# One vector sum of the SwiGLU weights queued behind an addition to a matmul bank

## The chip, the cores and the metric

The kernel runs on one core of a Trainium2 chip. A core has five engines that run side by side, each with its own queue worked off in order: TensorE (PE in the profile; its weight loads are PEld), VectorE (DVE), ScalarE (ACT), GpSimd (POOL) and SyncE (SP), which here issues most transfers. The metric is the time of one execution on the device in microseconds (us), lower is better.

## The reference, cut to what matters

One decoder block on 512 tokens of width 1024 in float32. Two token mixers (a gated convolution and a gated linear recurrence) are merged, and a SwiGLU channel mixer follows, with `D_FF = 2816`:

```python
x = x + m @ w_mix_out[l]
h = rmsnorm(x, norm2_g[l])
x = x + (jax.nn.silu(h @ ffn_w1[l]) * (h @ ffn_w3[l])) @ ffn_w2[l]
return rmsnorm(x, norm_f_g)
```

The change is in the products `h @ ffn_w1` and `h @ ffn_w3`.

## The kernel before, in words

**Products.** Float32 operands are split into a high part `h` and a low part `l`, and each product is made of three matmuls (high by high, low by high, high by low). Weights arrive by DMA in a buffer `raw`; ScalarE casts the high part (line 122) and VectorE, in this stage, subtracts to get the low part (line 118). Four `raw` buffers, two `wsum` buffers and five `hl` buffers (a split piece of weights) rotate.

**Seven products for eight.** The columns of `ffn_w1` and `ffn_w3` are worked in 11 pairs `k`, each pair being columns `j` and `j + 11` of both matrices in pieces of 128. Pair 0 is done plainly. The ten others use a scheme of the Strassen kind: the weights of a pair are seen as quarters `b11`, `b12`, `b21`, `b22`, and four sums of them, `t1` to `t4`, are made, so that seven products do (`b11`, `t1`, `b21`, `t2`, `t4`, `b22`, `t3`). Each product is 24 matmuls of 256 columns on line 1053. `f_sum` makes the sums in place: `t1 = b12 + b11` and `t2 = t1 + b22` by VectorE (line 346), `t3` by a subtraction, `t4` by an accumulating DMA that GpSimd issues (line 344).

**The banks.** The results meet in PSUM banks. The product `t1` is copied to a buffer `se`, the common sum, from its bank `fe` (line 1149). `t2` accumulates into the bank of `b11` (`fr` or `fa`), which is copied into a new bank `ft` (line 1144). Then `b22` accumulates into the old bank and `t3` into the new one. Behind `b22`, `se` is added to the old bank (line 1151, by the helper `add` of line 879). Behind `t3`, the bank is added to `se` (line 1153, same helper; in the profile `se<-ft,se`), and the result is gated by Silu on ScalarE (line 1110, `sl`) and a multiplication on VectorE (line 1111, into `ou` or `ov`). `t4` accumulates into the bank of `t3` and is gated likewise.

**The order.** The products are traced in this list, in which `t4` of a pair comes two products or so behind its `t3`, after the next pair has begun:

```python
for k, before in zip(F_PAIRS, [None] + F_PAIRS):
    F_ORDER += [(n, k) for n in ("b11", "t1", "b21", "t2") if n[0] == "t" or k not in BEGUN]
    if before is not None:
        F_ORDER.append(("t4", before))
    F_ORDER += [("b22", k), ("t3", k)]
F_ORDER.append(("t4", F_PAIRS[-1]))
```

For pairs 1 to 4 (`BEGUN`) the products `b11` and `b21` were done before this loop. Each product, when it asks for its weights, has the loads and sums of weights traced up to four pieces further on (`AHEAD = 4`); the sum `t1` is traced there, by `source` in `f_chunk`.

**Who orders the queues.** Outside a few stretches written by hand, a planner decides at build time the order of instructions in each engine's queue, from its own estimates of when each is ready. An instruction can be held behind another of the same engine by `tc.issue_after(ins)`, which fixes the order only and adds no wait for a result. `newest` is a dictionary of instructions for such edges; before the change it holds `load` and `sub`.

**Behind this stage** the products with `ffn_w2` follow (line 926, bank `or`), by the same scheme with `e`, `u`, `v` operands, with sums of weights that were made earlier and lie in DRAM (`os`). They end in the last norm and the store of the output.

Of the kernel before, what the change touches and what calls it, by code (L numbers as in the profile page):

```python
# [85 lines left out]
def tile_block(ctx, tc, a, out):  # L86
# [19 lines left out]
    def bank(name):  # L106
        return psum.tile([P, T], F32, tag="mm", name=name)
# [7 lines left out]
    newest = {}  # L115

    def sub(eng, o, x, y):
        return eng.tensor_tensor(out=o, in0=x, in1=y, op=ALU.subtract)  # L118
# [18 lines left out]
    def wchunk(key, src, kt, cols, where="hl", lo=pool_e, after=None):  # L137
        chunks.append((key, src, kt, cols, where, lo, after))
# [190 lines left out]
    def f_load(n, k, raw=None):  # L329
        if raw is None:  # L330
            p_, tag = (wsums, "wsum") if n in ("b12", "b22") else (raws, "raw")
            raw = p_.tile([P, 1024], F32, tag=tag, name=f"raw_f{n}_{k}")
        for i, w_ in enumerate((w1, w3)):
            nc.sync.dma_start(raw[:, i * T : (i + 1) * T].rearrange("p (k n) -> p k n", k=4), f_quarter(n, k, w_, 0, 4))
        f_raw[n, k] = raw

    def f_sum(n, k):

        o, x = {"t1": ("b12", "b11"), "t2": ("b12", "b22"), "t3": ("b11", "t2"), "t4": ("b21", "t2")}[n]
        q, y = f_raw[o, k], f_raw[x, k]  # L340
        if n == "t3":
            sub(vec, q, y, q)
        elif n == "t4" or k in ADDING:
            pool_e.dma_start(out=q, in_=y, accum_op=ALU.add)  # L344
        else:
            vec.tensor_tensor(out=q, in0=q, in1=y, op=ALU.add)  # L346
        f_raw[n, k] = q

    def f_chunk(n, k):

        again = k in BEGUN

        def source():
            if n in ("b11", "b21"):
                f_load(n, k)
                if n == "b11" and not again:
                    f_load("b12", k)
            elif n == "t1":
                for m in ("b11", "b12", "b22", "b21") if again else ("b22",):
                    f_load(m, k)  # L360
                f_sum("t1", k)
            return f_raw[n, k]

        def after(rv, h):
            if n == "t1":
                f_sum("t2", k)
                f_sum("t3", k)
                if again:
                    f_sum("t4", k)
            elif n == "b21" and not again:  # L370
                f_sum("t4", k)

        wchunk(f"f{n}_{k}", source, 8, P, "made", vec, after)
# [490 lines left out]
    for j in range(8):  # L864
        ws = w_tiles(f"lo{j}_0", 5) + w_tiles(f"lo{j}_1", 5)
        ps = bank(f"yb{j}")
# [12 lines left out]
    add = lambda o, x, y: vec.tensor_tensor(out=o, in0=x, in1=y, op=ALU.add)  # L879
# [100 lines left out]
    for n, j in enumerate(mixq.order()):  # L980
        ws = w_tiles(f"co{j}", ND)
        ps = bank(f"ya{j}")
# [64 lines left out]
    def f_product(ps, k, x_, w_, again=False, ahead=AHEAD):  # L1047

        h, l = weights(f"f{w_}_{k}", ahead)
        for i in range(2):  # L1050
            for c, (xh, xl) in enumerate(x_):
                for m, (lw, rx_) in enumerate(((h, xh), (h, xl), (l, xh))):
                    pe.matmul(  # L1053
                        ps[:, HALVES[i]], lw[:, 4 * i + c, :], rx_, start=not (again or i or c or m),
                        stop=bool(i and c == 3 and m == 2), skip_group_check=True,
                    )
# [51 lines left out]
    def f_out(c, dst, sign=1.0):  # L1108
        s_ = shortt("sl")
        act.activation(s_[:, LO], c[:, LO], AF.Silu, scale=sign)  # L1110
        vec.scalar_tensor_tensor(out=dst, in0=c[:, HI], scalar=sign, in1=s_[:, LO], op0=ALU.mult, op1=ALU.mult)
# [21 lines left out]
    def ffn_product(n, k):  # L1133

        b_ = seven.setdefault(k, {"a": first[k][0]} if k in BEGUN else {})
        x_ = {"b11": "a11", "b21": "a12", "b22": "s4", "t1": "s1", "t2": "s2", "t3": "s3", "t4": "a22"}[n]
        r = {"b11": "a", "b21": "b", "b22": "a", "t1": "e", "t2": "a", "t3": "c", "t4": "c"}[n]
        if n in ("b11", "t1"):
            b_[r] = (bank2 if r == "e" else bank)(f"f{r}_{k}")
        ps = b_[r]  # L1140
        f_product(ps, k, f_in[x_], n, n not in ("b11", "t1"))
        if n in ("b11", "t2"):
            new = b_["b" if n == "b11" else "c"] = bank(f"f{n}_{k}")
            act.copy(new, ps)
            if n == "b11":
                o7.uv[k] = longt(f"ou{k}"), longt(f"ov{k}")
        elif n == "t1":
            b_["se"] = shortt(f"se_{k}")
            act.copy(b_["se"], ps)
        elif n == "b22":  # L1150
            add(ps, ps, b_["se"])
        elif n == "t3":
            add(b_["se"], ps, b_["se"])
        if n not in ("b11", "t1", "t2"):
            i, cs = {"b21": (0, LO), "b22": (0, HI), "t3": (1, HI), "t4": (1, LO)}[n]
            f_out(b_["se"] if n == "t3" else ps, o7.uv[k][i][:, cs], -1.0 if n in ("b22", "t3") else 1.0)
        if n == "t4" and k >= SUMS_FROM:
            o7.pair(k - SUMS_FROM)

    for n, k in F_ORDER:  # L1160
        ffn_product(n, k)
# [95 lines left out]
```

## Time and profile before

| what | value |
| --- | --- |
| median of 3 runs | 806.26 us (805.32 to 806.38) |
| profiled execution | 806.61 us |
| its span, first to last instruction | 804.8 us |
| mean granted TensorE clock | 0.994 |
| busy: PE, DVE, ACT, POOL | 98%, 84%, 59%, 29% |
| sums of line 346 | 20, 1.23 us each, 493.2 to 663.8 us |
| additions `se<-ft,se` | 10, 0.68 us each, 522.9 to 689.8 us |

The profiled execution's own time is 1.8 us more than its span. The profile gives, for each instruction, its engine, line, operation, and the tiles that it writes and reads (`out<-in`), and for an idle time of an engine what released it. A chain of waits follows the work that ended last backwards, step by step. Matmuls are pipelined: the length shown for one (0.28 us for 256 columns) is longer than the distance from one to the next (0.12 us). The granted clock is the share of full speed that TensorE was given.

### The profile page before, as it was taken

The page shows a single profiled execution, that of the slowest core. Times are in us where ns is not written, and L with a number is a line of the kernel's source. Part 1 is how long each engine was busy: PE and PEld are TensorE (multiplying, and loading weights), DVE is VectorE, ACT ScalarE, POOL GpSimd, SP SyncE. Part 2 cuts the span into 40 slices and gives each one's busy share as a digit, 9 for nine tenths or more (in the row PEclk, how much of TensorE's full clock was granted, in tenths as well). Part 3 has the DMA queues.
Part 4 walks back from the last instruction along what each step waited for, and adds up shares of the span by engine and source line. Part 5 has one row for each costly group of instructions (what it writes and reads, how often), then busy time and mean ns, then how long its engine had stood idle before and what let it go on. Part 6 is the DMA issues. An engine that isn't in the chain of part 4 may idle for free.

```text
span 804.8 us, 12198 instructions
## 1 busy us (share of the span) xinstructions
PE 791.1 (98%) x4374; PEld 691.9 (86%) x4374; DVE 679.1 (84%) x1034; ACT 472.1 (59%) x677; POOL 232.3 (29%) x182
## 2 busy tenths in 40 slices
PE   8999999999999999999999999999999999999996
PEld 7988888788888888888888888998999999888885
DVE  5699899999989988787878889977778887899756
ACT  7546585988668855553326474544555555577443
POOL 3575866777766855030000000000000000000000
PEclk9999999999999999999999999999999999999999
DMA  7945646487564764469847545576555543676652
GB/s 214 235 133 152 188 139 208 119 240 204 166 208 140 210 180 119 128 217 273 283 135 236 158 132 157 132 200 166 132 132 132 132 132 105 206 261 200 198 170 104
DMA packets 184625, 140.29 MB, mean 174 GB/s; under 512 B 14280, under 2 KB 162164, under 8 KB 184564
## 3 DMA queue, kind: packets, MB, share of 16 engines
q1 hardware_dynamic: 183123, 134.27, 55.5%
q0 software_dynamic: 1440, 5.24, 3.5%
q8 instruction: 34, 0.56, 0.3%
q14 instruction: 28, 0.22, 0.1%
HBM read 113.79 MB, written 18.64 MB: 165 GB/s over the span
## 4 chain that ended last, share of the span: by engine, by line
PE 83%; DVE 10%; DMA 3%; ACT 2%; issue 1%; POOL 1%; SPq 0%; DVEq 0%; ACTq 0%; POOLq 0%
PE z L514 29%; PE or L926 13%; PE yb L514 7%; PE ft L1053 7%; PE fa L1053 6%; PE ya L514 5%; PE mxr L926 5%; PE fe L1053 3%; DVE cv L673 2%; PE fb L1053 2%; PE g L800 2%; PE fr L1053 2%; DMA raw_fb<-in_ffn_w_dram 1%; PE f L514 1%; DVE hl_ft L118 1%
## 5 line engine op out<-in xcount | busy, mean ns | idle before, releaser
L673 DVE SCALAR_TENSOR_TENSOR cv<-u,par,cv 128x511 f32<-128x511 f32 (+16 forms) x240 | 162.2, 730 | 2.7 <-ACT cv L670 2.5
L118 POOL TENSOR_TENSOR hl_in<-raw_in,hl_in 128x1024 fp32r<-128x1024 f32 x52 | 125.9, 2427 | 80.5 <-ACT hl_in L122 73.0
L344 POOL DMA_DIRECT2D raw_fb<-raw_fb x10 | 8.7, 875 | 303.1 <-DVE raw_fb L346 186.7
L118 POOL TENSOR_TENSOR ows<-ows 128x256 f32<-128x256 f32 x66 | 57.2, 869 | 37.5 <-DMA ows<-in_ffn_w_dram 34.6
L122 ACT CAST hl_in<-raw_in 128x1024 fp32r<-128x1024 f32 x52 | 54.2, 1043 | 9.6 <-PE z L514 6.5
L122 ACT CAST hl_ft<-raw_fb 128x1024 fp32r<-128x1024 f32 x40 | 41.9, 1049 | 29.5 <-DVE raw_fb L346 12.3
L118 DVE TENSOR_TENSOR hl_ft<-raw_fb,hl_ft 128x1024 fp32r<-128x1024 f32 x40 | 48.6, 1219 | 11.2 <-ACT hl_ft L122 11.1
L118 DVE TENSOR_TENSOR hl_fb<-raw_fb,hl_fb 128x1024 fp32r<-128x1024 f32 x30 | 36.6, 1221 | 10.6 <-ACT hl_fb L122 10.4
L514 PE MATMUL z<-h10h,hl_in 128*128 128x512 f32 (+1 forms) x112 | 42.4, 380 | 0.0
L514 PE MATMUL z<-h11h,hl_in 128*128 128x512 f32 (+1 forms) x112 | 41.8, 375 | 0.0
L514 PE MATMUL z<-h13h,hl_in 128*128 128x512 f32 (+1 forms) x112 | 41.8, 375 | 0.0
L514 PE MATMUL z<-h12h,hl_in 128*128 128x512 f32 (+1 forms) x112 | 41.8, 375 | 0.0
L514 PE MATMUL z<-h14h,hl_in 128*128 128x512 f32 (+1 forms) x112 | 41.8, 374 | 0.0
L514 PE MATMUL z<-h16h,hl_in 128*128 128x512 f32 (+1 forms) x112 | 41.7, 374 | 0.0
L514 PE MATMUL z<-h15h,hl_in 128*128 128x512 f32 (+1 forms) x112 | 41.7, 374 | 0.0
L514 PE MATMUL z<-h17h,hl_in 128*128 128x512 f32 (+1 forms) x112 | 41.7, 374 | 0.0
L346 DVE TENSOR_TENSOR raw_fb<-raw_fb,raw_fb 128x1024 f32<-128x1024 f32 x20 | 24.5, 1225 | 17.2 <-DMA raw_fb<-in_ffn_w_dram 16.9
L122 ACT CAST hl_fb<-raw_fb 128x1024 fp32r<-128x1024 f32 x30 | 31.4, 1047 | 6.8 <-PE mxr L926 3.7
L122 ACT CAST hl_ob<-raw_ob 128x1024 fp32r<-128x1024 f32 (+1 forms) x23 | 23.4, 1015 | 20.4 <-PE or L926 11.5
L118 DVE TENSOR_TENSOR hl_ob<-raw_ob,hl_ob 128x1024 fp32r<-128x1024 f32 (+1 forms) x23 | 27.0, 1174 | 9.6 <-ACT hl_ob L122 6.8
L1053 PE MATMUL fe<-hs_0h,hl_ft 128*128 128x256 f32 x160 | 30.8, 284 | 0.4 <-DVE hl_ft L118 0.4
L1053 PE MATMUL ft<-hs_1h,hl_ft 128*128 128x256 f32 x160 | 30.4, 283 | 0.0
(961 smaller groups left out, 2618.9 us busy)
## 6 DMA issues: line engine op xcount, KB each, us to landing
raw_in<-in_w_in_dram SPq DMA_DIRECT2D x52, 512.0 KB
raw_fb<-in_ffn_w_dram SPq DMA_DIRECT2D x96, 256.0 KB
ows<-in_ffn_w_dram SPq DMA_DIRECT2D x44, 256.0 KB
os<-ows SPq DMA_DIRECT2D x22, 512.0 KB
raw_ob<-in_ffn_w_dram SPq DMA_DIRECT2D x33, 256.0 KB
raw_ot<-os SPq DMA_DIRECT2D x33, 256.0 KB
raw_lo<-in_lru_w_out_dram SPq DMA_DIRECT2D x16, 320.0 KB
raw_fb<-raw_fb POOLq DMA_DIRECT2D x10, 512.0 KB, 4.6
```

The costliest lines, as they stand in the source:

```text
L118: return eng.tensor_tensor(out=o, in0=x, in1=y, op=ALU.subtract)
L122: copy(h, full)
L344: pool_e.dma_start(out=q, in_=y, accum_op=ALU.add)
L346: vec.tensor_tensor(out=q, in0=q, in1=y, op=ALU.add)
L514: pe.matmul(ps, l, r, start=i == 0, stop=i == n - 1)
L673: vec.scalar_tensor_tensor(out=acc[c][:, s:], in0=u[c][:, : T - s], scalar=dw(c, s), in1=acc[c][:, s:], op0=ALU.mult, op1=ALU.add)
L800: pe.matmul(ps, l, r, start=k == 0, stop=k == len(mms) - 1)
L926: pe.matmul(banks[i], l_[:, ts], r_, start=start and n == 0, stop=stop and n == 2, skip_group_check=again)
L1053: pe.matmul(ps[:, HALVES[i]], lw[:, 4 * i + c, :], rx_, start=not (again or i or c or m), stop=bool(i and c == 3 and m == 2), skip_group_c ...
```

## The change

The addition that ends `t3` is remembered in `newest["added"]`. When the sum `t1` of a pair is traced and such an addition is known, it is traced inside `tc.issue_after`, so that VectorE's queue has it behind that addition. The loads before it are outside the block.

```diff
             elif n == "t1":
                 for m in ("b11", "b12", "b22", "b21") if again else ("b22",):
                     f_load(m, k)
-                f_sum("t1", k)
+                if "added" in newest:
+                    with tc.issue_after(newest["added"]):
+                        f_sum("t1", k)
+                else:
+                    f_sum("t1", k)
             return f_raw[n, k]
...
         elif n == "t3":
-            add(b_["se"], ps, b_["se"])
+            newest["added"] = add(b_["se"], ps, b_["se"]).ins
```

## The prediction

> **What bounds the kernel now.** I read the page first, then the list of what TensorE waited for, then the chain of waits around the one large wait, then the timelines of VectorE and TensorE there, and last the granted clock by windows.
>
> ```profile
> span 804.8 us, 12198 instructions
> PE 791.1 (98%) x4374; PEld 691.9 (86%) x4374; DVE 679.1 (84%) x1034; ACT 472.1 (59%) x677; POOL 232.3 (29%) x182
> ```
>
> TensorE is busy 98% of the span: only time in which it stands still or runs slowly can be won. Its waits (total, times, longest):
>
> ```profile
> PE ft L1053 <- DVE se L879: 1.9, 1, 1.9
> PE g L800 <- DVE ext L118: 1.2, 1, 1.2
> ...
> PE fe L1053 <- DVE hl_ft L118: 0.4, 1, 0.4
> ```
>
> The largest single wait is for `se` on line 879, the helper `add`, and TensorE resumes on a tile `ft`. That is the addition that the change names. The chain of waits (start, length, what) shows what held it:
>
> ```profile
> 552.22 0.35 DVE ou L1111
> ...
> 552.69 3.63 DMA raw_fb<-in_ffn_w_dram
> ...
> 556.44 1.23 DVE raw_fb L346
> 557.67 0.61 DVE se L879
> 558.28 0.14 issue
> 558.41 4.61 PE ft L1053 x24
> 563.02 2.88 PE fr L1053 x24
> 565.90 2.88 PE ft L1053 x24
> 568.78 2.88 PE fa L1053 x24
> ```
>
> A load lands, VectorE does a sum of line 346 on it, then the addition, and only then does TensorE go on. The addition needs nothing from that sum; it merely stands behind it in VectorE's queue. The timeline of VectorE (start, length, instruction, idle before it):
>
> ```profile
> 551.00 1.22 DVE L118 TENSOR_TENSOR hl_fb<-raw_fb,hl_fb 128x1024 fp32r<-128x1024 f32 x1
> 552.14 0.42 DVE L1111 SCALAR_TENSOR_TENSOR ou<-fr,sl 128x256 f32<-128x256 f32 x1
> 556.44 1.23 DVE L346 TENSOR_TENSOR raw_fb<-raw_fb,raw_fb 128x1024 f32<-128x1024 f32 x1 [3.89 <-DMA raw_fb<-in_ffn_w_dram]
> 557.59 0.68 DVE L879 TENSOR_TENSOR se<-ft,se 128x512 f32<-128x512 f32 x1
> 558.19 1.22 DVE L118 TENSOR_TENSOR hl_ft<-raw_fb,hl_ft 128x1024 fp32r<-128x1024 f32 x1
> ```
>
> VectorE stood idle for 3.89 us with the addition queued behind. And TensorE:
>
> ```profile
> 550.50 0.28 PE L1053 MATMUL ft<-hs_1h,hl_ft 128*128 128x256 f32 x1
> ...
> 556.26 0.28 PE L1053 MATMUL fr<-hs_0h,hl_ft 128*128 128x256 f32 x1
> 558.41 0.36 PE L1053 MATMUL ft<-h24h,hl_ft 128*128 128x256 f32 x1 [1.88 <-DVE se L879]
> ...
> 562.86 0.28 PE L1053 MATMUL fr<-hs_1h,hl_fb 128*128 128x256 f32 x1
> ```
>
> The product that the addition reads (`t3` of pair 3) ended at 550.50 + 0.28 = 550.78. TensorE did `t1` and `t2` of pair 4 meanwhile, and then had to begin `t4` of pair 3, which accumulates into the bank that the addition reads.
>
> The stall has an aftermath. Windows (stretch, its length, busy time and instructions of PE, PEld, DVE, ACT, POOL, granted clock, DMA share, GB/s):
>
> ```profile
> 10.00:13.00 3.00, 3.00 (x16) 3.00 (x15) 2.92 (x8) 3.00 (x9) 2.13 (x1) 0.51 1.03 335
> 156.00:160.00 4.00, 2.76 (x13) 1.98 (x12) 3.94 (x5) 3.93 (x6) 4.00 (x3) 1.00 0.45 145
> 160.00:170.00 10.00, 10.00 (x44) 8.27 (x45) 10.00 (x17) 8.85 (x12) 9.71 (x9) 1.00 0.70 207
> 516.20:520.00 3.80, 3.79 (x31) 3.79 (x32) 3.77 (x4) 2.16 (x4) 0.86 (x1) 1.00 0.20 39
> 559.00:562.40 3.40, 3.40 (x19) 3.40 (x18) 2.67 (x4) 2.66 (x4) 0.00 (x0) 0.51 0.52 150
> 562.86:580.00 17.14, 17.14 (x145) 17.14 (x144) 13.56 (x17) 8.52 (x12) 0.86 (x1) 1.00 0.54 131
> ```
>
> For 3.4 us behind the stall the granted clock is 0.51, as at the kernel's start (10 to 13 us). Shorter gaps, of 4.00 - 2.76 = 1.24 us near 158 us and of 0.4 us near 516 us, are followed by 1.00.
>
> **The change part by part.** No instruction is added or removed: an order-only edge puts the first sum of a pair (`t1`, one vector addition of 128x1024) behind the newest traced `t3` addition. Weights are traced four products ahead. In the list of products `t1` of pair 5 stands at place 20, counted from 0; its sum is traced when product 16 (`t4` of pair 3) asks for its weights, and the newest `t3` then is that of pair 3, place 13. So the edge ties the sum of pair 5 behind the addition of pair 3, and later ones likewise with two pairs between. Pairs 1 and 2 are traced before any such addition and get no edge. For the others, VectorE's order now:
>
> ```profile
> 537.34 0.41 DVE L1111 SCALAR_TENSOR_TENSOR ou<-fr,sl 128x256 f32<-128x256 f32 x1
> 537.67 0.68 DVE L879 TENSOR_TENSOR se<-ft,se 128x512 f32<-128x512 f32 x1
> 541.07 1.23 DVE L346 TENSOR_TENSOR raw_fb<-raw_fb,raw_fb 128x1024 f32<-128x1024 f32 x1 [2.72 <-DMA raw_fb<-in_ffn_w_dram]
> ...
> 650.46 0.68 DVE L879 TENSOR_TENSOR se<-ft,se 128x512 f32<-128x512 f32 x1
> ...
> 656.76 1.23 DVE L346 TENSOR_TENSOR raw_fb<-raw_fb,raw_fb 128x1024 f32<-128x1024 f32 x1 [1.64 <-DMA raw_fb<-in_ffn_w_dram]
> ```
>
> Pair 4 (537.67 before 541.07) to pair 10 (650.46 before 656.76) already stand as the edge asks, except pair 5 (556.44 before 557.59). One swap of two neighbours is what the edge forces. Pair 4 shows the wanted form: gating product `ou`, addition, then the wait for the load.
>
> *The stall.* Swapped, the addition can follow `ou` at about 552.5 and end near 553.2 (0.68 long); its product was done at 550.78. TensorE needs it after its last matmul of 556.26 plus one matmul interval, 2.88/24 = 0.12, thus at 556.38: 3.1 us of cover. The stall goes: 558.41 - 556.38 = 2.03 us.
>
> *The slow clock.* From 558.41 to 562.86 the 24 matmuls took 4.45 us; at full clock such a product takes 2.88. If the slowdown follows from the stall, a further 1.57 us goes. I take it so: in the windows above, it comes right behind the longest gap and behind no short one.
>
> Together 3.60 us.
>
> *What the sum itself loses.* Nothing: it waits for a load that landed at 552.69 + 3.63 = 556.32, with the addition over by then. Behind it in the queue stands the split of `t3`'s weights of pair 4 (558.19 to 559.41), used by the product that starts at 565.90. It would move up by the addition's place, some 0.6 us, to end near 558.8, while its product moves to 565.90 - 3.60 = 562.3: 3.5 us of cover left. If the edge instead pushed the sum behind further work, each such instruction costs VectorE order, not work; 1.23 us, one more sum's length, stays inside that cover. The load's own release is `ou` or an instruction next to it; one addition later would be 0.7 us, also inside it. POOL's queue and SP's get no instruction more; the sums' stores and loads keep their order.
>
> *What is late next.* ScalarE: the copy of `t2`'s bank, which must be read before `b22` accumulates into it.
>
> ```profile
> 559.15 1.05 ACT L122 CAST hl_fb<-raw_fb 128x1024 fp32r<-128x1024 f32 x1
> 560.10 0.59 ACT L1144 COPY ft<-fr 128x512 f32<-128x512 f32 x1
> ```
>
> `b22` would start at 562.86 - 3.60 = 559.26. In ScalarE's order a cast of newly loaded weights comes ahead of the copy. If that cast waits for the same landing, it ends at 556.32 + 1.05 = 557.4 and the copy at 558.0: 1.3 us to spare. This is the thinnest cover near the swap, estimated from these rows.
>
> *The rest of the span.* From 563 us on TensorE has no wait left in the list above. In the output stage its lead is small:
>
> ```profile
> 706.14 1.23 DVE L118 TENSOR_TENSOR hl_ob<-raw_ob,hl_ob 128x1024 fp32r<-128x1024 f32 x1 [2.81 <-DMA x2b<-x2k]
> 734.77 1.22 DVE L118 TENSOR_TENSOR hl_ot<-raw_ot,hl_ot 128x1024 fp32r<-128x1024 f32 x1
> 737.50 0.61 PE L926 MATMUL or<-hl_ot,oeb0h 128*128 128x512 f32 x2
> SPq L263 <- DVE ov L1111: 12.2, 1, 12.2
> ```
>
> The split ends at 735.99, 1.5 us before its use. But the loads of that stage wait for VectorE's results (last row: SP's own wait), and those for TensorE's products, so I let the whole stage move by 3.60.
>
> The profiled execution took 806.61 us (span 804.8 and 1.8 around it): 806.61 - 3.60 = 803.0. The median of the runs is 806.26, 0.35 lower, which would give 802.7; I forecast 802.8, between the two.
>
> **Rivals.** *The stall goes, the slow stretch stays* (it has another cause than the gap): 2.03 us, 804.4. For it: the trace has one such case only. Against it: the clock is 1.00 everywhere else in the rows above behind the start. The Trainium skill, "TensorE: Matmul & The Clock Gate", section "What's actually happening", has the clock halve after at least one idle window of about 3.4 us; by that rule a gap of 2.03 us would be too short, and 804.4 the outcome. The trace agrees with its half rate (0.51) and its length (3.4 us), but not with the idle time needed. I give this 0.10, with smaller stalls that remain among it.
>
> *The gain is lost in the output stage*: if its loads, the landing before 706.14 first, keep their time, TensorE comes 3.60 us early to a lead of 1.5, stalls 2.1 and pays 1.57 for the clock: 806.2, no change. For it: VectorE has that stage full. Against it: the wait of SP for VectorE. With it goes the case that the planner keeps the old order. 0.10.
>
> *Slower*: the stall changes place to ScalarE's copy. The planner works out its order anew from the swap on; if it places a cast that waits for a later load ahead of the copy of `t2`'s bank, `b22` waits instead. The spare is 1.3 us; a stall of s behind it costs s + 1.57, so the kernel gets slower once the copy is more than 1.3 + 2.03 = 3.3 us late, and slower by 0.2% at 5 us late. A wait for a whole further transfer (3.63) behind a cast and a sum (1.05 and 1.23) is 5.9 us late: 4.6 + 1.57 - 3.60 = 2.6 us slower, 808.8. For it: a load held VectorE for 3.89 us in just this way. Against it: no such order in pair 4. 0.13.
>
> **How the numbers follow.** Full gain 0.67, about 802.0 to 803.6 (the runs' spread of 1.06 us about the forecast). Partial 0.10 at 804.4, unchanged 0.10 at 805.5 to 807, slower 0.13. About 0.2%, 1.6 us, is what a measurement tells from no change: faster means below 804.6. Full and partial give 0.77, less a little as 804.4 lies at the edge: faster 0.75, same 0.11, slower 0.14. The range, 801.9 to 806.0, takes in full, partial and part of the unchanged cases; the likeliest alone is 802.0 to 803.6.
>
> **What would show it.** Right: the addition of pair 3 starts near 552.5, ahead of the sum that still starts near 556.4; no TensorE wait for `se`; clock 1.00 from 556 to 563; `b22` of pair 4 at about 559.3; later products 3.6 us earlier and the last `or` matmul as well. Wrong: a wait of TensorE for line 1144 or for `hl_ft`, another window of 0.51, waits in the output stage, or the sum still ahead of the addition.

## The result and the profile after

The changed kernel took 804.51 us (median of 18 runs, 803.63 to 805.56), the kernel before beside it 806.49 us (18 runs, 805.13 to 808.09). The medians differ by 1.98 us. The ratio of the runs, with its 95% interval, is 0.9969 (0.9961 to 0.9978): faster by 0.31%, or 2.5 us (1.8 to 3.1). Both values are given below, since the difference between them is part of the uncertainty.

Only one queue is ordered differently, by two swaps of neighbours. In the traces the instructions of the two programs are in the same order on TensorE, ScalarE, GpSimd and SyncE. On VectorE the order before was `ou`, pair 5's sum, pair 3's addition, a split, and then the gating product `ov` of `se`:

```profile
559.32 0.42 DVE L1111 SCALAR_TENSOR_TENSOR ov<-se,sl 128x256 f32<-128x256 f32 x1
```

The order after is `ou`, the addition, the sum, `ov`, the split (rows below). The first swap, of pair 5's sum and pair 3's addition, is the one that the edge asks for; in the second, the planner put `ov` ahead of the split. In the profile after, lines behind the edit are numbered four higher. The page, and the two largest of TensorE's waits with the one of the product stage:

```profile
span 803.8 us, 12199 instructions
PE 790.0 (98%) x4374; PEld 690.7 (86%) x4374; DVE 678.6 (84%) x1034; ACT 471.8 (59%) x677; POOL 232.8 (29%) x182
```

```profile
PE g L804 <- DVE ext L118: 1.2, 1, 1.2
PE z L518 <- ACT hl_in L122: 1.2, 1, 1.2
...
PE fe L1057 <- DVE hl_ft L118: 0.5, 1, 0.5
```

The wait for `se` is gone, and no other took its place in this stage. VectorE's timeline after (start, length, instruction, idle before it):

```profile
555.48 0.42 DVE L1115 SCALAR_TENSOR_TENSOR ou<-fr,sl 128x256 f32<-128x256 f32 x1
555.82 0.68 DVE L883 TENSOR_TENSOR se<-ft,se 128x512 f32<-128x512 f32 x1
559.19 1.23 DVE L346 TENSOR_TENSOR raw_fb<-raw_fb,raw_fb 128x1024 f32<-128x1024 f32 x1 [2.69 <-DMA raw_fb<-in_ffn_w_dram]
560.33 0.42 DVE L1115 SCALAR_TENSOR_TENSOR ov<-se,sl 128x256 f32<-128x256 f32 x1
560.67 1.22 DVE L118 TENSOR_TENSOR hl_ft<-raw_fb,hl_ft 128x1024 fp32r<-128x1024 f32 x1
```

The addition now stands behind `ou`; VectorE waits for the load as before, and no wait of TensorE follows from it. The chain of waits there is TensorE alone, 2.88 us for each product, and the clock is full:

```profile
553.19 2.88 PE fe L1057 x24
556.07 2.88 PE fr L1057 x24
558.95 2.88 PE ft L1057 x24
```

```profile
546.00:580.00 34.00, 34.00 (x284) 33.87 (x283) 27.77 (x33) 18.39 (x27) 1.72 (x2) 1.00 0.64 164
```

In this pair of profiles the place gave the whole 3.60 us: from the first matmul of pair 3's `t3` to that of pair 4's `b22`, 562.86 - 547.74 = 15.12 us before and 561.67 - 550.15 = 11.52 us after. But the profiled executions differ by only 806.61 - 805.56 = 1.05 us. Most of the remainder lies ahead of the change. The first matmul of pair 3's `t3`, in TensorE's timeline of the kernel before and then of the changed one:

```profile
547.74 0.28 PE L1053 MATMUL ft<-hs_1h,hl_ft 128*128 128x256 f32 x1
```

```profile
550.15 0.28 PE L1057 MATMUL ft<-hs_1h,hl_ft 128*128 128x256 f32 x1
```

The profiled execution of the changed kernel came there 2.41 us later, though nothing ahead of it is ordered differently. Six profiles of the unchanged kernel show the same spread: this matmul starts at 547.74 to 550.17 us.

### The profile page after: what moved, and what is told of

It is laid out like the page before. It is cut to its first block, busy times and chain, and to the rows that moved or that the text cites. A ratio compares the mean times of both kernels' runs of the same rounds, so it can differ in the third digit from the quotient of the medians.

```text
span 803.8 us, 12199 instructions
## 1 busy us (share of the span) xinstructions
PE 790.0 (98%) x4374; PEld 690.7 (86%) x4374; DVE 678.6 (84%) x1034; ACT 471.8 (59%) x677; POOL 232.8 (29%) x182
## 4 chain that ended last, share of the span: by engine, by line
PE 82%; DVE 8%; DMA 4%; ACT 2%; SPq 1%; issue 1%; POOL 1%; ACTq 0%; POOLq 0%; DVEq 0%
PE z L518 28%; PE or L930 13%; PE ft L1057 7%; PE yb L518 7%; PE fa L1057 6%; PE ya L518 5%; PE mxr L930 5%; PE fe L1057 3%; PE fr L1057 3%; DVE cv L677 2%; PE fb L1057 2%; PE g L804 2%; DMA raw_in<-in_w_in_dram 2%; PE f L518 1%; DMA raw_fb<-in_ffn_w_dram 1%
```

## The experiments

**The unchanged kernel, five more profiles; the changed one, again.** If the stall costs 3.60 us in every execution, a gain of 2.5 us is too small. The first three profiles were taken beside a second timing of the changed kernel, with no edit to either.

> The kernel before, unchanged, for another profile. Theory A (the stall and the slow clock behind it come in every execution, 2.03 + 1.57 = 3.60 us, and the gain of the medians is smaller for another reason): TensorE waits 1.9 us for the addition near 556 us and the granted clock behind it is near 0.5 for 3.4 us. Theory B (the stall comes in every execution, the slow clock only in some): the same wait, but 4.45 us from the first matmul of the waiting product to the next product only in some profiles, 2.9 us in the others. Theory C (the stall itself varies, with the landing of the load): the wait differs by 0.5 us or more from profile to profile.

> As before_2: a third profile of the kernel before. A: wait 1.9 us and clock 0.5 behind it again. B: wait 1.9 us, clock 1.0 or 0.5. C: another wait.

> As before_2: a fourth profile of the kernel before. A: wait 1.9 us and clock 0.5 behind it again. B: wait 1.9 us, clock 1.0 or 0.5. C: another wait.

> The changed kernel again, timed in five rounds. A: 3.0 to 3.6 us under the kernel before, ratio 0.9955 to 0.9963. B and C: 2.0 to 2.6 us under it, ratio 0.9968 to 0.9975, and its own profile without a wait for the addition; the time from the start to the first product of pair 4 differs from the first profile of the changed kernel by up to 2.5 us, since nothing ahead of it was reordered.

The second timing: 804.59 us (12 runs, 803.74 to 805.51) against 806.15 us, ratio 0.9974 (0.9964 to 0.9984), which is 2.1 us (1.3 to 2.9); the medians differ by 1.56 us. In its profile TensorE has no wait for the addition, which stands at 553.09 ahead of the sum at 557.01, and the first product of pair 4 begins at 551.38 us, 1.65 earlier than in the first profile of the changed kernel. The single times of the three profiles of the kernel before were 805.67, 807.40 and 807.53 us. TensorE's wait in before_2, before_3 and before_4:

```profile
PE ft L1053 <- DVE se L879: 1.6, 1, 1.6
```

```profile
PE ft L1053 <- DVE se L879: 1.7, 1, 1.7
```

```profile
PE ft L1053 <- DVE se L879: 1.6, 1, 1.6
```

The chain of waits of before_2, and its granted clock behind the stall:

```profile
553.30 3.41 DMA raw_fb<-in_ffn_w_dram
...
556.84 1.22 DVE raw_fb L346
558.07 0.61 DVE se L879
...
558.81 3.10 PE ft L1053 x24
561.91 2.88 PE fr L1053 x24
```

```profile
558.81:564.00 5.19, 5.19 (x43) 5.19 (x44) 4.42 (x5) 4.52 (x7) 0.00 (x0) 1.00 0.57 160
```

The stall is there each time, by the same chain, but the waiting product then takes 3.10 us in this view, where the first profile had 4.61. The clock stayed full in all three. A is wrong. B fits these four profiles, with idle times of 1.56 to 1.88 us; C asks for a difference of 0.5 us. Two more profiles, taken later, were to decide between a threshold and the moment:

> A fifth profile of the kernel before; three of the four so far had the stall of 1.7 to 1.8 us with the clock at full speed behind it, one had 2.0 us and half rate. T (a threshold in length between 1.8 and 2.0 us): half rate only if the stall is 1.9 us or longer. M (the moment counts): half rate or not at a stall of 1.7 to 2.0 us, in about one profile of four.

> A sixth profile of the kernel before. T: half rate only if the stall is 1.9 us or longer. M: half rate in about one profile of four, at any stall of 1.7 to 2.0 us.

They took 810.00 and 809.26 us (the kernel before's own run beside them 807.3). TensorE's wait in before_5 and before_6:

```profile
PE ft L1053 <- DVE se L879: 2.8, 1, 2.8
```

```profile
PE ft L1053 <- DVE se L879: 2.1, 1, 2.1
```

The chain of before_5 and a window of it, and then the chain of before_6 and a window of it:

```profile
548.46 6.07 DMA raw_fb<-raw_fb
...
555.00 3.52 DMA raw_fb<-in_ffn_w_dram
...
558.64 1.23 DVE raw_fb L346
559.86 0.61 DVE se L879
...
560.61 5.46 PE ft L1053 x24
566.07 3.17 PE fr L1053 x24
```

```profile
560.61:564.40 3.79, 3.79 (x18) 3.79 (x19) 3.07 (x4) 3.23 (x5) 0.00 (x0) 0.50 0.59 170
```

```profile
561.04 4.24 PE ft L1053 x24
565.28 3.23 PE fr L1053 x24
```

```profile
561.04:566.00 4.96, 4.96 (x29) 4.96 (x30) 4.20 (x5) 3.87 (x7) 0.00 (x0) 0.66 0.54 154
```

Here the waits were 2.8 and 2.1 us, and the half rate followed both. It need not begin at once: in before_6 the matmuls start 0.12 us apart for 1.5 us behind the gap and only then 0.21 us apart, so the window's mean is 0.66. In before_5 the accumulating transfer for pair 4's `t4`, behind which SP issued the load, took 6.07 us in this chain (4.6 is the median from issue to landing in the first profile), so the load came late. The load stood behind this transfer in before_2 and before_6 too; in the first profile, before_3 and before_4 the chain puts it behind VectorE's work near `ou`. The cost of the stall, from the matmul starts (gap beyond 0.12 us, plus the next 48 matmuls beyond 5.76 us):

| profile of the kernel before | gap, us | slow clock, us | together, us |
| --- | --- | --- | --- |
| first | 2.03 | 1.57 | 3.60 |
| before_2 | 1.72 | 0.06 | 1.78 |
| before_3 | 1.82 | 0.06 | 1.88 |
| before_4 | 1.75 | 0.06 | 1.81 |
| before_5 | 2.94 | 2.71 | 5.65 |
| before_6 | 2.23 | 1.55 | 3.78 |

So C holds once before_5 and before_6 are counted (idle times of 1.56 to 2.78 us), and with it a step: a small change of the landing moves the gap, and a gap of 2.03 us or more was followed by the half rate, one of 1.82 us or less was not. The gains of the two timings, 2.5 and 2.1 us by the ratios, 2.0 and 1.6 us by the medians, lie at the lower end of this spread or just below it. The mean of the six profiles is 3.1 us, at the top of the first interval and just above the second. The closest match is within one session: before_2 to before_4, with 1.8 us, were taken beside the second timing. They ran on another chip (number 2) than before_5 and before_6 (15). How often an execution pays the slow clock, and whether the chip has a part in it, is not shown.

**The sum taken off VectorE instead.** The kernel before, in the old order, with pair 5's first sum made by a transfer. Only VectorE's and GpSimd's queues differ, by this one instruction.

```diff
-    ADDING = ()
+    ADDING = (5,)
...
-        elif n == "t4" or k in ADDING:
+        elif n == "t4" or (n == "t1" and k in ADDING):
             pool_e.dma_start(out=q, in_=y, accum_op=ALU.add)
```

> The kernel before, in the old order, with one difference: the first sum of pair 5 is made by an accumulating transfer that GpSimd issues instead of an addition on VectorE, so nothing on VectorE waits for that load. Theory S (the stall came from VectorE's queue standing at the sum's wait): no TensorE wait for the addition to se near 556 us, the addition about 6.5 us behind the start of its product as in the changed kernel, and the whole time like the changed kernel's, 1.5 to 2.5 us under the kernel before. Rival R (the swap won by something else, such as the order of the gating product and the split behind the sum, and the addition's wait was hidden anyway): no gain, within 0.5 us of the kernel before. Rival P (GpSimd's queue becomes late, since its transfers stand behind the new wait): TensorE waits for weights of pair 5, slower than the kernel before by 1 us or more.

808.64 us (12 runs) against 807.65 beside it, ratio 1.0013 (0.9997 to 1.0029). TensorE's one large wait, then the chain of waits, then VectorE's timeline:

```profile
PE fb L1053 <- ACT fb L1144: 3.9, 1, 3.9
```

```profile
554.45 0.61 DVE se L879
...
558.37 7.61 DMA raw_fb<-raw_fb
...
566.05 1.06 ACT hl_ft L122
...
574.28 0.61 DVE se L879
...
575.29 0.59 ACT fb L1144
575.93 4.57 PE fb L1053 x24
```

```profile
567.13 1.23 DVE L118 TENSOR_TENSOR hl_ft<-raw_fb,hl_ft 128x1024 fp32r<-128x1024 f32 x1 [8.89 <-ACT hl_ft L122]
```

S is right about the cause: with the sum gone from the queue, the addition follows `ou` at 554.45 and TensorE has no wait for it. S is wrong about the time. The interval, 0.2 us faster to 2.3 us slower, leaves room for the times of both R and P, but neither has the mechanism. The transfer took 7.61 us, so the split of the sum stood at the head of VectorE's queue for 8.89 us, with pair 4's addition behind it. That addition came at 574.28, its Silu held up ScalarE's copy of a bank (line 1144), and TensorE waited 3.9 us for the copy and ran behind it at half rate: in this profile 4.05 us of gap and 1.57 us of slow clock. A wait at the head of one queue was traded for a longer one, two queues further on. It is the line that the prediction named for its slower rival, but another copy (of the bank of pair 5's `b11`, not of a `t2`), held up in another way.

**The disputed cost by itself.** On the changed kernel, in-place copies ahead of the product `b21` open gaps on TensorE.

```diff
         if n in ("b11", "t2"):
             new = b_["b" if n == "b11" else "c"] = bank(f"f{n}_{k}")
             act.copy(new, ps)
             if n == "b11":
+                for _ in range(GAP.get(k, 0)):
+                    act.copy(new, new)
```

> The changed kernel with added work that opens a gap of its own on TensorE in each of pairs 5 to 10: 4, 5, 6, 7, 8 and 9 in-place copies of a bank on ScalarE ahead of the product b21 (the values stay the same). It measures the disputed cost by itself: what TensorE's clock does behind a gap. Theory T (a threshold in length): all gaps above some length between 1.3 and 2 us are followed by about 3.4 us at half rate and 1.6 us lost, none of the shorter. Theory M (the moment counts as well): gaps of 1.5 to 3 us are followed by the half rate only sometimes, longer ones mostly. Copies of 0.57 us each: gaps of some 0 to 3.5 us, the whole 8 to 20 us over the changed kernel.

> As gap_ramp, with six copies in each of the six pairs, so six gaps of nearly one length (some 1.2 to 2 us) at six moments in one execution. T: all of them or none are followed by the half rate. M: some are.

809.27 and 809.91 us, some 5 us over the changed kernel instead of 8 to 20, and hardly a gap: the planner put other products ahead of `b21`. One gap each, shown in TensorE's timeline of gap_ramp and then of gap_six (the last bracket is the idle time), both with the clock full behind them; gap_ramp had another of 0.48 us:

```profile
575.38 0.38 PE L1057 MATMUL fb<-h24h,hl_fb 128*128 128x256 f32 x1 [1.33 <-ACT fb L1152]
```

```profile
578.75 0.38 PE L1057 MATMUL fb<-h24h,hl_fb 128*128 128x256 f32 x1 [1.32 <-ACT fb L1152]
```

These two settle little. With TensorE's products held in the order of the list, the gaps came as wanted:

```diff
-        f_product(ps, k, f_in[x_], n, n not in ("b11", "t1"))
+        with tc.issue_after(newest["mm"]):   # the last matmul so far
+            f_product(ps, k, f_in[x_], n, n not in ("b11", "t1"))
```

> The changed kernel with TensorE's products of this stage held in the order of the list, and four in-place copies on ScalarE (values unchanged) ahead of the product b21 in each of pairs 5 to 10, so that TensorE has nothing else to do: six gaps of some 1 to 2 us. T: half rate behind those above 1.9 us only, each time. M: behind some of them and not others of the same length. The whole 6 to 15 us over the changed kernel.

> As gap_ordered_4 with five copies: six gaps of some 1.6 to 3 us. T: half rate behind every one above 1.9 us. M: behind some.

814.91 and 833.14 us. With four copies: the waits, and the first and last of six windows behind the gaps, all six at 1.00:

```profile
PE fb L1057 <- ACT fb L1153: 8.6, 6, 1.4
```

```profile
574.12:578.00 3.88, 3.88 (x32) 3.88 (x33) 2.21 (x2) 1.56 (x3) 0.00 (x0) 1.00 1.03 282
...
683.36:687.00 3.64, 3.64 (x30) 3.64 (x31) 1.22 (x1) 1.32 (x3) 0.00 (x0) 1.00 0.07 21
```

With five copies: the waits (4.1 once, and (18.5 - 4.1)/5 = 2.88 five times), the third of six windows at half rate, and the last, where it stayed away:

```profile
PE fb L1057 <- ACT fb L1153: 18.5, 6, 4.1
```

```profile
626.31:630.00 3.69, 3.69 (x17) 3.69 (x18) 1.85 (x2) 0.00 (x0) 0.00 (x0) 0.50 0.74 203
...
701.56:705.00 3.44, 3.44 (x28) 3.44 (x29) 0.72 (x1) 0.20 (x1) 0.00 (x0) 1.00 0.41 145
```

All idle times of 0.48 to 1.66 us at these two places (`ft` behind the addition, `fb` behind the copies), 12 in the profiles of the experiments, were followed by full speed. Of ten of 1.88 us and more (first profile, before_5, before_6, sum_by_dma, six here), nine were followed by the half rate, and one of 2.88 us was not. T is nearly right, with a border between 1.66 and 1.88 us of idle time in these profiles; the one exception leaves a part to M. What makes the exception is not shown.

The whole times agree with the price, as far as single runs can: 833.14 - 814.91 = 18.2 us, of which the longer gaps are 9.9 us and the slow clock 8.3 us, both from the matmul starts.

## Why the prediction was right or wrong

The forecast was 802.8 us in a range of 801.9 to 806.0; measured were 804.51 and 804.59. Faster was right, by 2.0 to 2.5 us in the first timing instead of some 3.6; the likeliest case's own range (802.0 to 803.6) was missed.

- *One swap of two neighbours*: right, but for the gating product `ov`, which came ahead of the split as well. That cost nothing.
- *The stall goes, 2.03 us*: right. The six profiles of the kernel before put it at 1.72 to 2.94 us.
- *The addition right behind `ou`, the sum still waiting for its load*: right (555.82, and 559.19 after 2.69 us of idle time). The cover was 558.79 - 556.50 = 2.3 us in this profile instead of 3.1.
- *Late next, ScalarE's copy of `t2`'s bank with 1.3 us to spare*: the copy was in time, but the working was not right. It assumed that the cast ahead of the copy waits for the sum's load. What held ScalarE before the change was the addition itself, through the Silu of `se` ahead of that cast:

```profile
558.36 0.42 ACT L1110 ACTIVATE sl<-se 128x256 f32<-128x256 f32 x1 [5.85 <-DVE se L879]
```

  After the change the cast began at 557.38, before the sum's load had landed, and the copy waited only for the product `t2`. It ended at 558.99 + 0.57 = 559.56, with `b22` from 561.67 on, so 2.1 us were left:

```profile
558.99 0.57 ACT L1148 COPY ft<-fr 128x512 f32<-128x512 f32 x1 [0.56 <-PE fr L1057]
```

- *The output stage moves with TensorE*: right. Its split and the product that uses it, after:

```profile
733.58 1.21 DVE L118 TENSOR_TENSOR hl_ot<-raw_ot,hl_ot 128x1024 fp32r<-128x1024 f32 x1
...
736.31 0.62 PE L930 MATMUL or<-hl_ot,oeb0h 128*128 128x512 f32 x2
```

  The lead is 736.31 - 734.79 = 1.5 us, as before.
- *The load's own release is `ou` or an instruction next to it*: so in three of the six profiles of the kernel before. In the other three it was the accumulating transfer, which is one way in which the stall varies.
- *The slow clock, 1.57 us*: this is the term that was mis-sized. Its cause was right (it follows the gap and went with it), and in the profiled execution it was there. But the sum was set against the median of the runs as if each had it; three of six profiles had 0.06 us instead, and the others 1.55 to 2.71. The gap sits near the border at which the clock drops, so a few tenths of a microsecond in a landing decide over 1.5 us. A stall of 1.8 us alone gives 806.5 - 1.8 = 804.7 us, next to what was measured. That the median execution pays no slow clock is inferred from this; no run counts it.
- *The rival with 804.4 us* (the slow stretch has another cause and stays) met the number without its mechanism. The changed kernel has no slow stretch there: it was the kernel before that often lacked it. The Trainium skill, "TensorE: Matmul & The Clock Gate", section "What's actually happening", asks for an idle window of about 3.4 us; here idle times of 1.88 to 2.88 us were enough in seven cases of eight, so the measurement decides against that figure for such gaps.
- *The slower rival*, and the loss in the output stage, did not come about.

## What to carry to other kernels

An instruction that waits for a load at the head of an in-order queue delays all that stands behind it (here the addition, and through it a Silu on ScalarE); look for the one behind it that another engine needs, and put that ahead. Moving the waiting instruction to a slower way of doing it can move the wait, as the sum by transfer showed. Before a stall of one profiled execution is set against a median, profile the same kernel a few times: here its cost was anything from 1.8 to 5.7 us.

## What the runs showed of the hardware

In this stage, where TensorE is otherwise busy throughout, its granted clock dropped to half behind idle times of 1.88 us and more (9 of 10) and not behind those of 1.66 us and less (12 of 12). The drop cost 1.4 to 1.6 us beside the gap, twice 2.7 us. An accumulating transfer of 512 KB that GpSimd issued took 4.6 us in the median, but 6.07 and 7.61 us in two chains of waits. The time until pair 3's `t3` begins varied by 2.4 us between executions with the same order of work ahead of it.
